# The start of a hybrid decoder layer: two weight loads split on VectorE alone, and 18 transposes of the identity on TensorE

## The chip, the cores and the metric

The kernel runs on one core of a Trainium2 chip. The metric is the device time of one execution in microseconds (us); the time before is the median of three runs.

## The reference, cut to what matters

One layer over 512 tokens of width 1024, float32: token mixing with two groups of heads that share one input projection, then cross-attention, then a squared-ReLU MLP. The change lies in the first lines of the mixing:

```python
h = rmsnorm(x, norm_mix_g[l])
proj = h @ w_in[l]
p_qn, p_qr, p_ckv, p_kr, p_qi, p_ki, p_wi, p_qkv = jnp.split(proj, split_at, axis=-1)
...
c_kv = rmsnorm(p_ckv, kv_norm_g[l])
k_rope = rope(p_kr[:, :, None, :])[:, :, 0]
q_idx = rope(p_qi.reshape(B, S, IDX_HEADS, IDX_DIM))
k_idx = rope(p_ki[:, :, None, :])[:, :, 0]
```

The latent keys `c_kv`, the small rotary keys, the index keys and index weights (232 columns together) come first, then the 512 index queries. They feed the indexer, whose top-128 choice of keys restricts the attention of group A.

## The kernel before, in words

The 512 tokens are four tiles of 128 rows. Each float32 operand of a product is split into a high part `hi` (a cast on ScalarE, line 130 for weights, 230 for activations) and a rest `lo` (a subtraction, line 131 or 231), and a product is made of three passes: hi by hi, hi by lo, lo by hi (`mm3`, line 107 issues them). Eight row blocks of 128 make the inner dimension, so one tile's product has 24 steps.

`load_weight` fetches a weight in units into the tag `wraw` (three buffers), splits each into `whi` and `wlo` (six buffers each), and takes a letter for each unit that says on which engine the subtraction runs: "p" is GpSimd and "v" VectorE, with the cast on ScalarE in both. A weight of at most 256 columns has two units of four row blocks, a wider one four units of two row blocks.

The start goes as follows. GpSimd makes the identity. SP issues the first rows of x, the gains, the first weight `wa` (232 columns, two units) with the remaining rows between its units, then tables, then the second weight `wb` (512 columns, four units). For each token tile, eight transposes (line 113) put its columns into PSUM, lines 230 and 231 make the two parts of `hT`, and line 267 sums the squares of the row (`junk`), from which GpSimd gets `r_mix` (line 200). Then for each tile the product with `wa` is made in a bank of the tag `mm` (three buffers) and evacuated: a mean square on ScalarE (line 205), `rk` on GpSimd (line 200), `ctok`, eight rotary products (line 289), two sums (line 296), a copy and `weff` on VectorE, and three transposes that are split into `cT`, `kiT` and `krT`. Then the query products with `wb` for tiles 1 to 3 in the same banks, their rotary products, and the index products, whose relu is weighted and summed on VectorE (lines 375 and 377). Further on come the weights of group B (`wv` with "vpvp", queries and keys with "pppp"), the choice of the top 128 (lines 557 and 558, VectorE), the two attentions, the cross-attention and the MLP. The bank of the tag `pv` (one buffer) is first used by the attention of group B.

The order on each engine isn't written out here: a planner simulates the engines with costs of its own and takes of the ready instructions the one that comes first in the program. Each engine then runs its list in that order. Only later parts (from the output projection on) hold TensorE to the program's order.

Of the kernel before, what the change touches and what calls it, by code (L numbers as in the profile page):

```python
# [17 lines left out]
P = 128  # L18
# [5 lines left out]
NH = 8  # L24
DH = 64
DR = 32
# [12 lines left out]
C_QN, C_QR, C_CKV, C_KR, C_QI, C_KI, C_WI, C_QB, C_KB, C_VB = (  # L39
    0, 512, 768, 896, 928, 1440, 1504, 1512, 2024, 2536)  # L40
# [24 lines left out]
def kernel(  # L65
# [16 lines left out]
    def nm(s):  # L82
        uid[0] += 1
        return f"{s}_{uid[0]}"

    def mtile(shape, dt, tag, bufs=1, pool=None):
        return (pool or main).tile(shape, dt, name=nm(tag), tag=tag, bufs=bufs)

    def small(tag, n=1):
        return main.tile([P, n], F32, name=nm(tag), tag=tag, bufs=8)  # L90

    def bank(tag, bufs):
        return psp.tile([P, 512], F32, name=nm(tag), tag=tag, bufs=bufs)
# [18 lines left out]
    def tpose(*a, **k):  # L112
        ins = nc.tensor.transpose(*a, **k)  # L113
        if ordered[0]:
            tc.keep_in_program_order(ins)

    ident = main.tile([P, P], F32, name="ident")
# [6 lines left out]
    def split_unit(raw, hi, lo, how="v"):  # L124


        if how in "PV":
            nc.vector.tensor_copy(hi, raw)  # L128
        else:
            nc.scalar.copy(hi, raw)  # L130
        (nc.gpsimd if how in "pP" else nc.vector).tensor_tensor(lo, raw, f32(hi), op=ALU.subtract)  # L131

    def load_weight(w, segs, k0, how, between=None):


        n = sum(c1 - c0 for c0, c1 in segs)
        nk = 4 if n <= 256 else 2
        his, los = [], []
        for u in range(KD // nk):
            raw = mtile([P, nk, n], F32, "wraw", 3)  # L140
            hi = mtile([P, nk, n], F32R, "whi", 6)
            lo = mtile([P, nk, n], F32R, "wlo", 6)
            rows = w[(k0 + nk * u) * P:(k0 + nk * u + nk) * P, :].rearrange("(k p) c -> p k c", p=P)
            o = 0
            for c0, c1 in segs:
                nc.sync.dma_start(raw[:, :, o:o + c1 - c0], rows[:, :, c0:c1])
                o += c1 - c0
            split_unit(raw, hi, lo, how[u % 4])
            if between is not None:
                between(u)  # L150
            for j in range(nk):
                his.append(hi[:, j, :])
                los.append(lo[:, j, :])
        return his, los
# [44 lines left out]
    def rstd_of(mean_eps, dst):  # L199
        nc.gpsimd.tensor_tensor(dst, mean_eps, mhalf, op=ALU.pow)  # L200
# [19 lines left out]
    def transpose_half(rows, g0, his, los, bank=bank_tp):  # L220

        tps = [bank()[:, :2 * P].rearrange("p (j t) -> p j t", j=2) for _ in range(2)]
        for i in range(2):
            for j in range(2):
                tpose(tps[i][:, j, :], rows[:, (2 * i + j) * P:(2 * i + j + 1) * P], ident)
        for j in range(2):
            for i in range(2):
                c = 2 * i + j
                g = gT[:, g0 + c:g0 + c + 1]
                nc.scalar.activation(his[c], tps[i][:, j, :], AF.Copy, scale=g)  # L230
                nc.vector.scalar_tensor_tensor(los[c], tps[i][:, j, :], g, f32(his[c]), op0=ALU.mult, op1=ALU.subtract)  # L231
# [3 lines left out]
    att = p1b.enter_context(tc.tile_pool(name="att", bufs=1, side="right"))  # L235
    tmp = p1a.enter_context(tc.tile_pool(name="tmp1", bufs=1))

    xa = [mtile([P, 2, D], F32, f"u2{c}") for c in "ab"]
    nc.sync.dma_start(xa[0][:, 0, 0:512], x_rows[:, 0, 0:512])
    load_gains([norm_mix_g], G_MIX)  # L240
    nc.sync.dma_start(xa[0][:, 0, 512:], x_rows[:, 0, 512:])
    w_in0 = w_in[0]

    def x_load(t):
        nc.sync.dma_start(xa[t // 2][:, t % 2, :], x_rows[:, t, :])

    wa = load_weight(w_in0, [(C_CKV, C_KR + DR), (C_KI, C_WI + NH)], 0, "vpvp", between=lambda u: x_load(1 + u))
    x_load(3)
    tabs = tmp.tile([P, CONST_COLS - 640], F32, name="tabs")
    nc.sync.dma_start(tabs, consts[:, 640:])  # L250
# [7 lines left out]
    for t in range(NT):  # L258
        xt = xa[t // 2][:, t % 2, :]
        tsl = slice(t * P, (t + 1) * P)  # L260
        for h in range(2):
            transpose_half(xt[:, 512 * h:512 * h + 512], G_MIX + 4 * h,
                           [hT[0][:, 4 * h + j, tsl] for j in range(4)],
                           [hT[1][:, 4 * h + j, tsl] for j in range(4)], (bank_tp, bank_s)[h])
        junk = att.tile([P, D], BF16, name=nm("junk"), tag="p", bufs=3)
        ss = small("ss")
        nc.vector.tensor_tensor_reduce(junk, xt, xt, op0=ALU.mult, op1=ALU.add, scale=1.0 / D, scalar=EPS, accum_out=ss)
        rstd_of(ss, r_mix[:, t:t + 1])
# [69 lines left out]


    qiT = mtile([P, NH, 3, P], F32R, "u1")  # L340
    wb = load_weight(w_in0, [(C_QI, C_QI + 512)], 0, "pppp")
    for t in range(1, NT):
        ps = bank_mm()
        mm3(ps, h_tok(t), wb)
# [19 lines left out]
    for b in range(1, NT):  # L364
        n = P * (b + 1)
# [630 lines left out]
```

## Time and profile before

| what | value |
|---|---|
| median of three runs | 813.85 us (813.5 to 816.56) |
| profiled execution, its own time | 814.07 us |
| its span, first to last instruction | 812.3 us |
| TensorE products busy | 785.9 us, 97% |
| VectorE busy | 560.0 us, 69% |
| ScalarE busy | 382.5 us, 47% |
| GpSimd busy | 215.4 us, 27% |

The engines are PE (TensorE products), PEld (its weight loads), DVE (VectorE), ACT (ScalarE), POOL (GpSimd) and SP (the queue that issues most transfers). Times in the trace count from the start of the span. A busy share is a mean over the whole span. A timeline row gives the start, the time from the start of the first to the end of the last instruction merged into it, the engine, the line, the operation, what it writes and reads, its shape and its count; the brackets give the idle time before it and what ended it. `whi`, `wlo` and `wraw` are the parts of a weight, `h` both parts of `hT`.

### The profile page before, as it was taken

Reading aid. Unit: us, or ns where it says so; the run is one execution under the profiler, and the core shown is the slowest. Engines: PE = TensorE matmul, PEld = TensorE weight load, DVE = VectorE, ACT = ScalarE, POOL = GpSimd, SP = SyncE. Lnnn points to the kernel's source line nnn. Section 1 sums busy time; section 2 is a strip of 40 time slices with the busy share of each in tenths; the row PEclk is TensorE's granted clock in tenths of the full one; section 3 lists DMA queues with packets and bytes.
Section 4 is the critical chain, followed back from the end, with each engine's and each line's share of the span. In section 5 each row is a group of like instructions: output and inputs, shape, how many; then the busy total and the mean of one; then the engine's idle time right before and its main releaser. Section 6 shows DMA issues by size and latency. Waiting matters only on the chain.

```text
span 812.3 us, 11144 instructions
## 1 busy us (share of the span) xinstructions
PE 785.9 (97%) x4066; PEld 649.0 (80%) x4066; DVE 560.0 (69%) x1169; ACT 382.5 (47%) x743; POOL 215.4 (27%) x164
## 2 busy tenths in 40 slices
PE   6799999999999999999999999999999999999995
PEld 5688878985698778788898888888888888888884
DVE  6775999998668844634683447767776776676674
ACT  5444333457955634222472545533552455345544
POOL 4733143130613406544510201110111011201132
PEclk9899999999999999999999999999999999999998
DMA  8441232202423303322540333496439743963482
GB/s 288 133 119 38 69 105 73 66 1 78 156 79 105 105 1 103 102 80 79 181 140 18 103 104 82 101 229 212 99 83 209 225 100 85 223 221 85 89 164 103
DMA packets 53223, 94.12 MB, mean 116 GB/s; under 512 B 5265, under 2 KB 11057, under 8 KB 53169
## 3 DMA queue, kind: packets, MB, share of 16 engines
q1 hardware_dynamic: 44464, 76.64, 30.1%
q0 software_dynamic: 8704, 16.78, 12.4%
q8 instruction: 32, 0.52, 0.3%
q14 instruction: 23, 0.18, 0.1%
HBM read 90.78 MB, written 2.10 MB: 114 GB/s over the span
## 4 chain that ended last, share of the span: by engine, by line
PE 82%; DVE 10%; issue 3%; POOL 2%; ACT 2%; DMA 1%; SPq 0%; POOLq 0%; ACTq 0%; DVEq 0%
PE mm L107 61%; PE sc L107 11%; PE tp L113 5%; PE pv L107 3%; PE tp L107 2%; DVE glo L558 1%; DVE m L557 1%; DVE ghi L377 1%; ACT whi L130 1%; DMA u2b<-in_w_down_dram 1%; DVE whi L128 1%; DVE rb L289 1%; DVE kk L296 0%; DMA u2a<-in_x_dram 0%; DVE wlo L131 0%
## 5 line engine op out<-in xcount | busy, mean ns | idle before, releaser
L131 POOL TENSOR_TENSOR wlo<-wraw,whi 128x1024 fp32r<-128x1024 f32 (+2 forms) x59 | 139.3, 2379 | 186.8 <-ACT whi L130 156.7
L107 PE MATMUL mm<-whi,h 128*128 128x512 f32 (+2 forms) x536 | 165.3, 377 | 6.9 <-DVE h L231 3.5
L130 ACT CAST whi<-wraw 128x1024 fp32r<-128x1024 f32 (+3 forms) x111 | 114.0, 1029 | 93.9 <-PE mm L107 42.4
L107 PE MATMUL mm<-h,whi 128*128 128x512 f32 (+1 forms) x448 | 153.2, 366 | 0.0
L107 PE MATMUL mm<-u,whi 128*128 128x512 f32 x320 | 125.0, 390 | 0.0
L107 PE MATMUL mm<-u,wlo 128*128 128x512 f32 x320 | 124.7, 390 | 0.0
L107 PEld LDWEIGHTS mm<-whi,h 128*128 128x128 f32 x536 | 100.6, 194 | 21.6 <-DVE h L231 3.9
L107 PE MATMUL mm<-wlo,h 128*128 128x512 f32 (+2 forms) x280 | 104.9, 376 | 0.1
L131 DVE TENSOR_TENSOR wlo<-wraw,whi 128x1024 fp32r<-128x1024 f32 (+1 forms) x64 | 80.6, 1260 | 29.7 <-ACT whi L130 29.4
L107 PEld LDWEIGHTS mm<-h,whi 128*128 128x128 f32 x448 | 80.7, 188 | 14.7 <-issue 1.2
L895 POOL DMA_DIRECT2D u2b<-in_w_down_dram x24 | 32.6, 1369 | 224.5 <-DMA wraw<-in_w_down_dram 120.6
L107 PE MATMUL mm<-whi,ghi 128*128 128x512 f32 x192 | 76.2, 397 | 0.0
L107 PE MATMUL mm<-wlo,ghi 128*128 128x512 f32 x192 | 75.7, 394 | 0.0
L107 PE MATMUL mm<-whi,glo 128*128 128x512 f32 x192 | 75.1, 391 | 0.0
L107 PEld LDWEIGHTS mm<-u,wlo 128*128 128x128 f32 x320 | 60.1, 188 | 12.5
L107 PEld LDWEIGHTS mm<-u,whi 128*128 128x128 f32 x320 | 60.1, 188 | 12.2
L131 DVE TENSOR_TENSOR wlo<-u2b,whi 128x1024 fp32r<-128x1024 f32 x32 | 39.1, 1225 | 30.2 <-ACT whi L130 30.2
L107 PEld LDWEIGHTS mm<-wlo,h 128*128 128x128 f32 x280 | 54.1, 194 | 7.2 <-DVE wlo L131 0.5
L130 ACT CAST whi<-u2b 128x1024 fp32r<-128x1024 f32 x32 | 33.6, 1052 | 48.0 <-DMA u2b<-in_w_down_dram 39.5
L428 ACT ACTIVATE p<-p,mx 128x128 f32<-128x128 f32 (+3 forms) x64 | 35.9, 563 | 26.4 <-DVE mx L426 26.3
L862 ACT ACTIVATE sq<-r 128x512 f32<-128x512 f32 x32 | 20.2, 631 | 49.1 <-DVE r L860 49.1
L860 DVE SCALAR_TENSOR_TENSOR r<-mm,rT 128x512 f32<-128x512 f32 x32 | 22.0, 688 | 30.3 <-PE mm L107 23.2
(250 smaller groups left out, 1433.7 us busy)
## 6 DMA issues: line engine op xcount, KB each, us to landing
wraw<-in_w_up_dram SPq DMA_DIRECT2D x32, 512.0 KB, 4.7
wraw<-in_w_down_dram SPq DMA_DIRECT2D x24, 512.0 KB, 6.1
u2b<-in_w_down_dram POOLq DMA_DIRECT2D x24, 512.0 KB, 7.6
wraw<-in_w_in_dram SPq DMA_DIRECT2D x16, 512.0 KB, 4.0
wraw<-in_w_kv_cross_dram SPq DMA_DIRECT2D x16, 512.0 KB, 3.7
wraw<-in_w_out_dram SPq DMA_DIRECT2D x8, 512.0 KB, 3.8
wraw<-in_w_q_cross_dram SPq DMA_DIRECT2D x8, 512.0 KB, 3.7
wraw<-in_w_o_cross_dram SPq DMA_DIRECT2D x8, 512.0 KB, 3.7
```

The lines of the kernel that those rows point to most:

```text
L107: ins = nc.tensor.matmul(*a, **k)
L113: ins = nc.tensor.transpose(*a, **k)
L128: nc.vector.tensor_copy(hi, raw)
L130: nc.scalar.copy(hi, raw)
L131: (nc.gpsimd if how in "pP" else nc.vector).tensor_tensor(lo, raw, f32(hi), op=ALU.subtract)
L289: nc.vector.scalar_tensor_tensor(o, i, r, tab, op0=ALU.mult, op1=ALU.mult)
L377: nc.vector.scalar_tensor_tensor(acc[b], rl[:, :n], wh, acc[b], op0=ALU.mult, op1=ALU.add)
L428: nc.scalar.activation(pr[:, c], pr[:, c], AF.Exp, bias=mx[:, i:i + 1], scale=-1.0, accum_out=sm[:, i:i + 1])
L557: nc.vector.max(m8, acc[b])
L860: nc.vector.scalar_tensor_tensor(r, ps, 0.0, rows_ready[0], op0=ALU.max, op1=ALU.mult)
L862: nc.scalar.activation(sq, r, AF.Square)
L895: nc.gpsimd.dma_start(xw[:, u], src, accum_op=ALU.add)
```

## The change

`load_weight` for `wa` and for `wb` gets "v" for every unit. A bank of the tag `pv` is taken at the start, and `busy(n)` writes n transposes of the identity into its four quarters in turn: 10 before the first rows are asked for in the program's order, and 8 after the transposes of token tile 0. Nothing reads that bank.

```diff
@@ -235,6 +235,14 @@
     tmp = p1a.enter_context(tc.tile_pool(name="tmp1", bufs=1))
+    idle = bank("pv", 1)
+
+    def busy(n):
+        for i in range(n):
+            tpose(idle[:, (i % 4) * P:(i % 4 + 1) * P], ident, ident)
+
+    busy(10)
     xa = [mtile([P, 2, D], F32, f"u2{c}") for c in "ab"]
@@ -244,7 +252,7 @@
-    wa = load_weight(w_in0, [(C_CKV, C_KR + DR), (C_KI, C_WI + NH)], 0, "vpvp", between=lambda u: x_load(1 + u))
+    wa = load_weight(w_in0, [(C_CKV, C_KR + DR), (C_KI, C_WI + NH)], 0, "vvvv", between=lambda u: x_load(1 + u))
@@ -262,6 +270,8 @@
                            [hT[1][:, 4 * h + j, tsl] for j in range(4)], (bank_tp, bank_s)[h])
+        if t == 0:
+            busy(8)
         junk = att.tile([P, D], BF16, name=nm("junk"), tag="p", bufs=3)
@@ -338,7 +348,7 @@
-    wb = load_weight(w_in0, [(C_QI, C_QI + 512)], 0, "pppp")
+    wb = load_weight(w_in0, [(C_QI, C_QI + 512)], 0, "vvvv")
```

## Rows read from the trace of the kernel before

**Rows 1.** What TensorE waited for, 0 to 60 us: total, times, longest.
```profile
PE tp L113 <- DMA u2a<-in_x_dram: 3.7, 1, 3.7
PE mm L107 <- DVE h L231: 3.5, 1, 3.5
...
PE mm L107 <- DVE weff L329: 1.0, 1, 1.0
```

**Rows 2.** Busy time by stretch: us, PE, PEld, DVE, ACT, POOL, clock, DMA, GB/s.
```profile
80.00:180.00 100.00, 98.49 (x541) 83.81 (x541) 98.62 (x296) 42.06 (x93) 32.87 (x18) 1.00 0.23 65
180.00:215.00 35.00, 32.98 (x192) 19.79 (x189) 27.48 (x88) 28.41 (x73) 8.47 (x4) 0.96 0.33 99
```

**Rows 3.** The same view in slices of one microsecond.
```profile
24.00:25.00 1.00, 0.00 (x0) 0.00 (x0) 1.00 (x4) 0.09 (x1) 0.79 (x2) 0.60 0.92 338
...
30.00:31.00 1.00, 1.00 (x7) 0.99 (x6) 0.22 (x1) 0.62 (x2) 0.86 (x2) 0.50 0.00 0
```

**Rows 4.** The timeline of TensorE, 0 to 30 us.
```profile
5.14 1.11 PE L113 MATMUL sc<-ident,u2a 128*128 128x128 f32 x4
8.45 0.56 PE L107 MATMUL mm<-whi,h 128*128 128x232 f32 x1 [2.19 <-ACT whi L130]
...
12.10 0.42 PE L107 MATMUL mm<-wlo,h 128*128 128x232 f32 x1
...
14.19 0.28 PE L107 MATMUL mm<-wlo,h 128*128 128x232 f32 x1
...
25.55 0.56 PE L107 MATMUL mm<-whi,h 128*128 128x232 f32 x1 [3.46 <-DVE h L231]
...
27.39 0.42 PE L107 MATMUL mm<-wlo,h 128*128 128x232 f32 x1
```

**Rows 5.** The timeline of VectorE, 10 to 36 us, and one row at 75 us.
```profile
11.65 3.16 DVE L267 CUSTOM_DVE_ANT_0 junk<-u2b 128x1024 bf16<-128x1024 f32 x1
...
15.00 1.23 DVE L267 CUSTOM_DVE_ANT_0 junk<-u2b 128x1024 bf16<-128x1024 f32 x1
...
18.86 0.35 DVE L321 SCALAR_TENSOR_TENSOR ctok<-mm,rk,gkvr 128x128 f32<-128x128 f32 x1 [0.45 <-POOL rk L200]
...
20.33 0.35 DVE L231 SCALAR_TENSOR_TENSOR h<-tp,gT,h 128x128 fp32r<-128x128 f32 x1
20.59 4.03 DVE L296 TENSOR_TENSOR kk<-kk,rb 128x64 f32<-128x64 f32 x2
...
34.47 1.22 DVE L131 TENSOR_TENSOR wlo<-wraw,whi 128x1024 fp32r<-128x1024 f32 x1
35.60 0.35 DVE L296 TENSOR_TENSOR kk<-kk,rb 128x64 f32<-128x64 f32 x2
...
75.01 2.44 DVE L377 SCALAR_TENSOR_TENSOR glo<-rl,weff,glo 128x256 f32<-128x256 f32 x1 [2.53 <-ACT rl L372]
```

**Rows 6.** The timeline of GpSimd, 0 to 31 us.
```profile
1.01 0.28 POOL masks.py:199 TENSOR_SCALAR_AFFINE_SELECT ident<-ident 128x128 f32<-128x128 f32 x1
...
11.58 2.15 POOL L131 TENSOR_TENSOR wlo<-wraw,whi 128x928 fp32r<-128x928 f32 x1
...
19.91 4.66 POOL L131 TENSOR_TENSOR wlo<-wraw,whi 128x1024 fp32r<-128x1024 f32 x2
...
27.96 2.37 POOL L131 TENSOR_TENSOR wlo<-wraw,whi 128x1024 fp32r<-128x1024 f32 x1 [3.09 <-ACT whi L130]
30.29 0.57 POOL L200 TENSOR_TENSOR rk<-rstd,mhalf 128x1 f32<-128x1 f32 x1
```

**Rows 7.** The chain that ended last, at the first query product: start, us, what.
```profile
34.70 5.72 PE mm L107 x24
```

**Rows 8.** SP's queue, a row of the timeline from 20 to 33 us.
```profile
22.30 8.42 SPq L146 DMA_DIRECT2D wraw<-in_w_in_dram  x3
```

**Rows 9.** The page: a group of part 5, and part 6 (KB each, us to landing).
```profile
L130 ACT CAST whi<-wraw 128x1024 fp32r<-128x1024 f32 (+3 forms) x111 | 114.0, 1029 | 93.9 <-PE mm L107 42.4
...
wraw<-in_w_in_dram SPq DMA_DIRECT2D x16, 512.0 KB, 4.0
```

## The prediction, made before the kernel was timed

> **What bounds the kernel now.** I read the page first, then the list of what TensorE waits for, the long table by stages, the one-microsecond table of the start, and last each engine's own order there. The page's busy shares are means over stages with different limits, so they say little about a change in the start. The list of waits says where TensorE's idle time is: of what it waits for in the first 60 us, nearly all comes before 35 us: 3.7 us for the first rows, 3.5 us for a VectorE instruction, 1.0 us for a bank [rows 1], and 2.2 us for the first weights [rows 4]. From 80 to 180 us it idles 1.5 us, from 180 to 215 us 2.0 us [rows 2]. There is something to gain in the first 35 us, then, and it reaches the end only if the stretch from 80 to 215 us doesn't take it back.
>
> In the first 35 us the reader should see three things. First, TensorE is slow up to about 14 us and again from 25.5 to 31 us. The clock column shows the second stretch: it falls within the slice 24 to 25 us, after TensorE has idled since about 22 us, and is still at 0.50 (1.2 GHz) from 30 to 31 us. A product of 232 columns with "wlo" takes 0.42 us there (27.39). At 12.10 it also takes 0.42 us, and at 14.19 0.28 us [rows 3, 4]. The column shows nothing of the first stretch; I trust the length of the products and put the rise between 12.1 and 14.2 us.
>
> Second, the 3.5 us of idle time hang on one VectorE pair, the sums "kk" of line 296. It lasts 4.03 us at 20.59, and 0.35 us at 35.60. It ends at 24.6 us, when GpSimd's two subtractions of line 131, begun at 19.91, end. The row sum "junk" at 11.65 lasts 3.16 us, at 15.00 only 1.23 us; a GpSimd subtraction ran from 11.58 to 13.73 us there [rows 5, 6]. A VectorE instruction that reads PSUM, line 231 at 20.33, ran through.
>
> Third, the bank that TensorE waits for at 34.70 us becomes free with "weff" of token tile 1 [rows 1, 7]. That evacuation needs tile 1's "rk" from GpSimd, which starts at 30.29 us, right behind the subtraction of 27.96 us [rows 6].
>
> **What the change removes.** "wa" has only two units (232 columns go four row blocks at a time), so "vpvp" held one GpSimd split; "wb" held four. Five subtractions leave GpSimd: one of 2.15 us, two of 4.66 us together, and two of about 2.37 us, 11.6 us in all [rows 6]. With them go, on VectorE, the surplus at the two blocked places: 3.16 - 1.23 = 1.9 us and 4.03 - 0.35 = 3.7 us, 5.6 us together [rows 5]. VectorE gets five subtractions: the one at 34.47 lets the next instruction start 1.13 us later, so four such are 4.5 us and one of 928 in place of 1024 columns is 1.0 us, 5.5 us together [rows 5]. VectorE's total stays as it is; what changes is its order, and TensorE's idle time and clock.
>
> The Trainium skill, page "SBUF — State Buffer", section "SBUF: two separate sides", says that VectorE and GpSimd share one pair of ports under an exclusive lock, which a VectorE instruction with two SBUF inputs needs too. The rows of lines 296 and 267 agree, and by that rule both blocked places vanish.
>
> TensorE's side. Without the block, 3.5 us of idle time go. The stretch from 25.55 to 31.0 us, busy at half rate, gives 2.7 us back. The bank wait gives up to 1.0 us. If the clock rises before the first product at 8.45 us, what is done until 12.1 or 14.2 us takes half: 1.8 to 2.9 us if TensorE is busy all that time [rows 1, 3, 4]. I take 2.4 us; that makes 9.6 us as the upper end.
>
> VectorE's side. By 11.65 us it has finished tile 0's eight "h" and one of tile 1. Before tile 1's "weff" it must still do two row sums (2.4 us at 1.2), the second "wa" split (1.0), 23 "h" of line 231 at 0.26 us (20.33 to 20.59; 6.0), tile 0's evacuation and that of tile 1 up to weff. From ctok at 18.86 us to the end of the eight rotary products at 20.33 us it is 1.47 us; the two sums add 0.35 us, and a copy and two small splits 0.8 us if I cost them like an "h". So tile 0 takes 2.6 us, and tile 1 1.6 us with weff [rows 5]. The sum is 13.6 us, which gives 25.3 us at the earliest, against 34.5 us now: 9.2 us gained. If all four "wb" splits come ahead of weff, it is 29.8 us: 4.7 us gained. The planner fills VectorE's idle time with them, so some will come ahead: I take two, 2.3 us, and the 0.45 us that VectorE waited for tile 0's rk [rows 5]. That is 28.1 us, a gain of 6.4 us, below TensorE's upper end, so VectorE sets it.
>
> The raw buffers. "wraw" has three, so the fourth "wb" unit is fetched when the first has been split: the first of the two merged GpSimd splits ends at 22.2 us, and SP goes on at 22.30 [rows 6, 8]. From there it is 4.0 us to landing, 1.03 us for the cast [rows 9] and 1.13 us for the split: 6.2 us. The query product needs that unit after 18 of its 24 steps, which take 5.72 us: 4.3 us after its start [rows 7]. If VectorE has split the first unit by 26 us, a product begun at 28.1 us waits for nothing.
>
> What is added. Ten transposes need only the identity, ready at 1.3 us [rows 6]. Four took 1.11 us at 5.14 us, some 0.4 us of it the last one's own length, so about 0.23 us each [rows 4]: ten end at 3.6 us, before the first rows at 3.75 us [rows 1]. The other eight, 1.8 us, fit into the idle time before 8.45 us (2.2 us). If the planner puts them ahead of tile 0, which needs its rows while they need none, tile 0's transposes come up to 1.8 us later, and the same 2.2 us cover that. I take nothing, and bound it by 0 and 1.8 us. Their bank, "pv", is used next by the attention of group B, far behind on the same engine. If they don't raise the clock, they cost nothing under this cover and bring nothing.
>
> The Trainium skill, page "TensorE: Matmul & The Clock Gate", Part 4, says that transposes don't count as TensorE activity for its clock in the way products do; it speaks against this part. No stretch of this trace holds transposes alone for long enough to tell. By that rule the 2.4 us fall out, and 7.2 us are left as TensorE's upper end.
>
> **The sum.** The profiled execution took 814.07 us (its span of 812.3 us and 1.8 us around it), 0.2 us above the median of 813.85 us. Off go 6.4 us at the start of the query products. I give back 1.1 us: the two "wb" splits left for later are 2.3 us of VectorE's time inside TensorE's query products, and I let half of it become waits. Gain 5.3 us, so 808.5 us from the median. From the query products on TensorE has almost no idle time up to 180 us, so the shift is carried. The likeliest case's own range is 804.6 us (9.2 us gained) to 810.5 us (4.7 us, less the leak and a little for order).
>
> **Rivals.**
> 1. The transposes don't lift the clock. A "wlo" product still takes 0.42 us up to about 12 us. Of 2.4 us I count 2.0 us as lost, since VectorE limits that stretch too: 810.5 us. For it speaks only the absence of a row to the contrary.
> 2. VectorE becomes the bound: all four splits come ahead of weff, or the first comes so late that the fourth unit's 6.2 us end behind the query product. Then the gain is 4.7 us less about 2.3 us of new waits: 811.5 us. For it: VectorE has few microseconds to spare there; against it: "h" and evacuations come first in the program.
> 3. The gain is taken back later. VectorE is busy 98.6 of 100 us between 80 and 180 us [rows 2]. If its work in there doesn't start earlier, TensorE waits the more for it between 180 and 215 us: 813.9 us. Against it: that work starts from index products of TensorE, which move forward with the rest.
> 4. Slower: the blocking moves instead of going. GpSimd keeps two splits of "wv" and all of the query and key weights of group B, and an index sum at 75.01 us, 256 columns wide, is held 2.44 us as it is [rows 5]. If the new order lets these splits meet VectorE's two-input work more often, VectorE has its 5.5 us more and no relief, with 1.4 us free from 80 to 180 us [rows 2]. TensorE then comes out of that stretch up to 5.5 us late: 819.4 us. It decides from about 4 us of new blocking on.
>
> **Chances.** Forecast 0.55, rival 1 0.12, rival 2 0.13, rival 3 0.12, rival 4 0.08. About 0.5% (4.1 us) is what a measurement of this kernel tells from no change, so faster means under 809.8 us. Of the forecast 0.50 lies there, of rival 1 0.05; rivals 2 and 3 and what is left of these two lie within; slower takes rival 4 and 0.01 of rival 3. That is 0.55, 0.36 and 0.09. The range takes in the upper end of the gain and rival 3, and leaves out rival 4 and the edges: 804.8 to 814.2 us.
>
> **What would show it.** Right: no wait over 1 us for a VectorE "h" in the first 30 us; no 0.50 in the clock column there; a "wlo" product of 0.28 us at 10 us already; the pair of line 296 under 0.5 us throughout; the first query product of 512 columns at 25 to 30 us. Wrong: that product later than 32 us, a fall of the clock while TensorE waits for splits, or TensorE's idle time between 180 and 215 us grown by what the start gained. The weakest step is the count of splits put ahead of weff, since that order is the planner's.

## The result and the profile after

| | before | after |
|---|---|---|
| median of 8 runs each, us | 814.59 (813.46 to 816.56) | 822.90 (815.14 to 824.92) |
| ratio, with its 95% interval | | 1.0078 [1.0059, 1.0097] |
| profiled execution, us | 814.07 | 823.06 |
| its span, us, and mean granted clock | 812.3, 0.990 | 821.3, 0.979 |

The kernel became slower by 0.8%; 808.5 us was forecast, in a range of 804.8 to 814.2. After's eight runs aren't spread evenly. Two, with a mean clock of 0.990 and 0.992, took 816.95 and 815.14 us; the other six, with 0.978 to 0.982, took 822.65 to 824.92 us. The profiled execution is one of the six.

**The start.** What TensorE waited for from 0 to 60 us of after (total, times, longest), to be held against [rows 1]:

```profile
PE tp L113 <- DVE h L231: 2.5, 4, 1.0
PE mm L107 <- ACT h L230: 2.2, 1, 2.2
PE pv L113 <- POOL ident masks.py:199: 1.4, 1, 1.4
```

The waits of 3.7 us for rows, of 3.5 us for one VectorE "h" and of 1.0 us for "weff" are gone. The wait for rows only gave way to the transposes of the identity: tile 0's own transposes come later, at 5.24 us instead of 3.75. What is left for "h" comes in pieces of at most 1.0 us, and VectorE's timeline in after shows why (start, us):

```profile
13.29 1.21 DVE L277 CUSTOM_DVE_ANT_0 junk<-u2b 128x1024 bf16<-128x1024 f32 x1
...
17.56 1.23 DVE L131 TENSOR_TENSOR wlo<-wraw,whi 128x1024 fp32r<-128x1024 f32 x1 [0.29 <-ACT whi L130]
...
21.57 1.22 DVE L131 TENSOR_TENSOR wlo<-wraw,whi 128x1024 fp32r<-128x1024 f32 x1
...
23.22 0.21 DVE L306 TENSOR_TENSOR kk<-kk,rb 128x64 f32<-128x64 f32 x1
...
23.97 1.22 DVE L131 TENSOR_TENSOR wlo<-wraw,whi 128x1024 fp32r<-128x1024 f32 x1
...
25.47 1.21 DVE L131 TENSOR_TENSOR wlo<-wraw,whi 128x1024 fp32r<-128x1024 f32 x1
...
29.10 0.21 DVE L339 TENSOR_SCALAR weff<-mm,r_mix 128x8 f32<-128x8 f32 x1
```

The row sum takes 1.21 us where it took 3.16, the pair "kk" 0.21 (at 23.22) and 0.18 us (at 23.61) where it took 4.03 [rows 5]. That is what the Trainium skill, page "SBUF — State Buffer", section "SBUF: two separate sides", would have, and this trace agrees. All four "wb" splits stand ahead of weff. TensorE's timeline in after:

```profile
1.35 4.10 PE L113 MATMUL pv<-ident 128*128 128x128 f32 x18 [1.35 <-POOL ident masks.py:199]
5.24 0.54 PE L113 MATMUL tp<-ident,u2a 128*128 128x128 f32 x3
...
6.03 0.60 PE L113 MATMUL sc<-ident,u2a 128*128 128x128 f32 x4
8.80 0.56 PE L107 MATMUL mm<-whi,h 128*128 128x232 f32 x1 [2.17 <-ACT h L230]
...
10.71 0.41 PE L107 MATMUL mm<-wlo,h 128*128 128x232 f32 x1
...
29.62 0.39 PE L107 MATMUL mm<-whi,h 128*128 128x512 f32 x1
```

The planner put all 18 transposes ahead of tile 0's. Behind them four transposes of rows take 0.60 us (at 6.03), where four took 1.11 us in before [rows 4]: the engine ran fast by then, though it had done nothing but transposes. Then it idles 2.17 us, and the first products are as slow as before (0.56 us; "wlo" 0.41 us at 10.71). One-microsecond slices of after (columns as in [rows 2]) show it, and a second fall like the one in [rows 3]:

```profile
8.00:9.00 1.00, 0.20 (x1) 0.20 (x1) 0.49 (x1) 1.00 (x4) 0.00 (x0) 0.87 1.16 353
9.00:10.00 1.00, 0.67 (x2) 0.40 (x3) 1.00 (x3) 0.59 (x4) 0.00 (x0) 0.50 1.07 367
...
26.00:27.00 1.00, 1.00 (x7) 1.00 (x6) 1.00 (x3) 0.39 (x2) 1.00 (x1) 0.50 0.75 94
```

**How much the start gained.** The first query product of 512 columns begins at 29.62 us instead of 34.70 [rows 7], 5.1 us earlier. But that overstates it, as TensorE's groups of instructions up to that product show. Before, up to 34.69 us:

```profile
L107 PE MATMUL mm<-whi,h 128*128 128x232 f32 x64 | 17.5, 353 | 5.9 <-DVE h L231 3.5 <-ACT whi L130 2.2 <-ACT h L230 0.2
L107 PE MATMUL mm<-wlo,h 128*128 128x232 f32 x32 | 10.1, 323 | 0.1
...
L113 PE MATMUL sc<-ident,u2b 128*128 128x128 f32 x8 | 2.0, 346 | 0.0
```

After, up to 29.61 us:

```profile
L107 PE MATMUL mm<-whi,h 128*128 128x232 f32 x50 | 13.9, 362 | 2.4 <-ACT h L230 2.2 <-DVE h L231 0.2
L107 PE MATMUL mm<-wlo,h 128*128 128x232 f32 x26 | 8.7, 337 | 0.3 <-DVE wlo L131 0.3
...
L113 PE MATMUL sc<-ident,u2b 128*128 128x128 f32 x6 | 1.4, 330 | 0.6 <-DVE h L231 0.6
```

Of 96 products with "wa" only 76 lie ahead of it: 20 were moved behind. So were six transposes, two of the last rows and the first two each of "ctok" and, in its two widths, "kk". At 0.11 us each at full rate (two products from 29.28 to 29.50 us, a transpose of "ctok" from 34.16 to 34.27) these 26 are 2.9 us. By this estimate the start gained about 2.2 us.

**Where it goes.** The next milestone is the last of the index products with 256 columns, which starts VectorE's work on the choice of the top 128. In before it begins at 74.12 us, in after at 77.94. The same view up to those times, before (to 74.1 us):

```profile
L107 PE MATMUL mm<-whi,h 128*128 128x512 f32 x102 | 33.4, 396 | 1.0 <-DVE weff L329 1.0
L107 PE MATMUL mm<-wlo,h 128*128 128x512 f32 x51 | 20.3, 398 | 0.0
```

and after (to 77.9 us):

```profile
L107 PE MATMUL mm<-whi,h 128*128 128x512 f32 x119 | 38.3, 395 | 0.0
L107 PE MATMUL mm<-wlo,h 128*128 128x512 f32 x60 | 23.6, 393 | 0.0
```

TensorE does 179 products of 512 columns before it, where it did 153. 72 of them are query products in both; the others are products for group B, which the program has behind the index products. The planner took 81 of these first in before already, all with "wv", and 107 in after: the 96 with "wv" and 11 with the next weight (by the lists that e5 and e6 hold, below). At 5.72/24 = 0.24 us [rows 7] the 26 more are 6.2 us: 6.2 less the 2.2 gained is 4.0, and 3.8 us is measured. VectorE's work on the top 128 starts 2.8 us late and ends 8.6 us late, as its first and last "m" show, before:

```profile
79.89 0.43 DVE L557 MAX8 m<-glo 128x8 f32<-128x256 f32 x1
...
179.68 0.69 DVE L557 MAX8 m<-ghi 128x8 f32<-128x512 f32 x1
```

and after:

```profile
82.66 0.43 DVE L567 MAX8 m<-glo 128x8 f32<-128x256 f32 x1
...
188.23 0.67 DVE L567 MAX8 m<-ghi 128x8 f32<-128x512 f32 x1
```

Ahead of its last rounds after does scores of group B's attention on VectorE (line 436, from 185.03 us on) that before has behind them (line 426, from 185.51 us on). The same stretches as in [rows 2], of after, and the one behind them:

```profile
80.00:180.00 100.00, 97.11 (x548) 82.96 (x547) 98.93 (x289) 41.94 (x94) 30.44 (x17) 1.00 0.21 59
180.00:215.00 35.00, 32.54 (x149) 18.75 (x148) 25.24 (x84) 22.47 (x58) 3.42 (x2) 0.76 0.21 61
215.00:250.00 35.00, 33.91 (x254) 27.12 (x253) 24.28 (x87) 24.50 (x66) 10.90 (x5) 0.95 0.37 121
```

VectorE has as little free time as before (1.1 us of 100), so it doesn't make up its delay; TensorE idles 2.9 us there instead of 1.5. In the second stretch the clock column falls from 0.96 to 0.76: 0.20 x 35 = 7.0 us of full-rate work. In slices of two microseconds, after:

```profile
184.00:186.00 2.00, 0.77 (x3) 0.50 (x4) 2.00 (x8) 1.42 (x4) 0.00 (x0) 1.00 0.94 175
186.00:188.00 2.00, 2.00 (x7) 0.97 (x6) 2.00 (x9) 1.25 (x5) 0.00 (x0) 0.56 0.95 253
...
196.00:198.00 2.00, 2.00 (x6) 0.72 (x4) 0.91 (x3) 0.00 (x0) 0.00 (x0) 0.50 0.00 0
...
202.00:204.00 2.00, 2.00 (x8) 0.73 (x8) 1.10 (x5) 2.00 (x7) 0.00 (x0) 0.67 0.00 0
```

TensorE is busy 0.77 of the 2 us before 186 us, then the clock falls to 0.50 and stays there about 17 us, although TensorE is busy. The wait in front of the fall is one for VectorE (TensorE's timeline of after), in the first scores of the attention:

```profile
184.15 0.41 PE L113 MATMUL mm<-ident,ghi 128*128 128x128 f32 x2 [0.46 <-DVE rb L299]
185.64 1.09 PE L107 MATMUL sc<-u2b,u2a 64*128 64x384 f32 x2 [1.08 <-DVE mx L436]
```

In before the same product begins behind 0.49 us of waiting for "mx", and its slice from 184 to 186 us is busy 1.31 us. The first scores themselves aren't late (182.78 us, in before 183.98): TensorE had done other work ahead. So the loss is best counted on TensorE, as an estimate from the rows above. From 80 to 250 us it idles 2.9 us more than before (1.4, 0.4 and 1.1; before has none in the third stretch) and loses 8.8 us more to the clock (7.0, and 0.05 x 35 = 1.8). Less the 2.2 us that the start gained, that is 9.5 us, near the 9.0 us by which the span grew. The clock is the greater part by far.

### The profile page after: what moved, and what is told of

Same layout as the page of the kernel before. It is cut to its first block, busy times and chain, and to the rows that moved or that the text cites. A ratio compares the mean times of both kernels' runs of the same rounds, so it can differ in the third digit from the quotient of the medians.

```text
span 821.3 us, 11197 instructions
## 1 busy us (share of the span) xinstructions
PE 796.3 (97%) x4084; PEld 655.2 (80%) x4084; DVE 560.7 (68%) x1174; ACT 383.9 (47%) x743; POOL 204.0 (25%) x159
## 4 chain that ended last, share of the span: by engine, by line
PE 70%; DVE 19%; issue 4%; DMA 3%; ACT 2%; POOL 1%; SPq 0%; POOLq 0%; ACTq 0%
PE mm L107 50%; PE sc L107 11%; PE tp L113 4%; DVE m L567 3%; PE pv L107 2%; DVE ghi L568 2%; PE tp L107 2%; DMA u2b<-in_w_down_dram 2%; DVE rb L299 2%; DMA wraw<-in_w_in_dram 1%; DVE ghi L387 1%; DVE tok L299 1%; DVE wlo L131 1%; DVE glo L568 1%; DVE tok L306 1%
## 5 line engine op out<-in xcount | busy, mean ns | idle before, releaser
L131 POOL TENSOR_TENSOR wlo<-wraw,whi 128x1024 fp32r<-128x1024 f32 (+1 forms) x54 | 127.3, 2374 | 198.8 <-ACT whi L130 168.2
L107 PEld LDWEIGHTS mm<-whi,h 128*128 128x128 f32 x536 | 99.8, 194 | 16.5 <-ACT h L230 2.6
L131 DVE TENSOR_TENSOR wlo<-wraw,whi 128x1024 fp32r<-128x1024 f32 (+2 forms) x69 | 86.9, 1260 | 31.0 <-ACT whi L130 31.0
L107 PEld LDWEIGHTS mm<-u,whi 128*128 128x128 f32 x320 | 60.1, 188 | 12.3
```

The lines of the kernel that those rows point to most:

```text
L107: ins = nc.tensor.matmul(*a, **k)
```

## The experiments

Three theories were open when the trace of after had been read. **Theory 1:** the gain at the start is real, and the planner's other order of TensorE's instructions takes it back. **Theory 2:** the transposes cost it. **Theory 3:** VectorE's five added subtractions are the loss, whatever the order. "Q" is the start of the first query product, "I" that of the last index product of 256 columns, both in the profiled execution. The kernel before ran beside each group of kernels: 815.04 us beside the first four, 815.33 beside the next four, 815.53 beside the last three (medians of 29). e2 has six runs, e6 five, e8 eleven, the others twelve each.

| kernel | median, us | ratio to before, 95% | Q, us | I, us | I - Q |
|---|---|---|---|---|---|
| before | | | 34.70 | 74.12 | 39.4 |
| after | 822.90 | 1.0078 [1.0059, 1.0097] | 29.62 | 77.94 | 48.3 |
| e1_wa_only | 811.81 | 0.9974 [0.9953, 0.9995] | 30.74 | 70.16 | 39.4 |
| e2_wb_only | 822.12 | 1.0091 [1.0075, 1.0107] | 26.51 | 76.75 | 50.2 |
| e3_splits_only | 820.85 | 1.0055 [1.0032, 1.0078] | 27.65 | 77.33 | 49.7 |
| e4_busy_only | 815.88 | 1.0018 [1.0004, 1.0032] | 33.09 | 74.59 | 41.5 |
| e5_splits_old_order | 812.95 | 0.9964 [0.9942, 0.9985] | 30.98 | 70.42 | 39.4 |
| e6_before_new_order | 827.67 | 1.0143 [1.0112, 1.0175] | 32.04 | 84.11 | 52.1 |
| e7_after_old_order | 817.26 | 1.0022 [1.0001, 1.0042] | 34.22 | 73.66 | 39.4 |
| e8_after_bridge | 816.24 | 1.0008 [0.9991, 1.0024] | 35.57 | 75.02 | 39.5 |
| e9_bridge_all_order | 814.87 | 0.9988 [0.9968, 1.0008] | 32.05 | 71.47 | 39.4 |
| e10_wb_one_unit | 813.64 | 0.9977 [0.9959, 0.9996] | 32.95 | 72.37 | 39.4 |
| e11_wb_two_units | 823.27 | 1.0087 [1.006, 1.0114] | 29.44 | 77.86 | 48.4 |

The last column is the one to read first. Where TensorE has before's list from there on, 39.4 to 39.5 us lie between the two products whatever else is changed; where it has the one with 26 more products ahead, 48.3 to 52.1. (e4's list is one product shorter than before's there; its 41.5 us hold 5 us at a clock of 0.50.) VectorE follows: from its first "m" to its last it is 99.7 to 99.8 us with the first kind of list, and 105.6 to 105.7 us with the second (e4: 103.9).

**The parts, each alone.** e1 changes the letters of "wa", e2 those of "wb", e3 both, and e4 adds only the transposes (the edits here and below are shortened).

```diff
 e1, e3:  wa = load_weight(..., 0, "vpvp" -> "vvvv", ...)
 e2, e3:  wb = load_weight(..., 0, "pppp" -> "vvvv")
 e4:      idle, busy(n), busy(10), busy(8) as in the change; "vpvp" and "pppp" stay
```

> Only the second unit of the 232-column weight goes to VectorE; the query weight stays on GpSimd, and there are no transposes of the identity. TensorE's list is then the one of before, instruction for instruction. If the loss comes from the new order of TensorE's list (theory 1), this kernel has none of it: 812 to 814.6 us, at most 2 us faster, because one of the two blocked places of VectorE (the row sum at 11.65 us) goes. If the loss comes from the transposes (theory 2), the same. If VectorE's added work is the loss (theory 3): 1 us slower, about 815.5 us.

> Only the query weight goes to VectorE. TensorE's list then has the index products of the first block behind some 13,300 more columns of other products than before (125,184 columns ahead of the eighth in place of 111,872; the change has the same). Theory 1 (order): the first query product comes at 29 to 31 us, 4 to 5 us earlier, but the eighth index product at 76 to 79 us, no earlier than the 74 us of before; time 814 to 823 us, not faster. Theory 2 (the transposes cost it): 808 to 811 us. Theory 3 (VectorE's added 4.5 us): about 819 us wherever the index products stand.

> Both splits as in the change, none of the transposes. Theory 1: as the run with the query weight alone, whose TensorE order it shares at the index products: 813 to 823 us. Theory 2: 808.5 us as forecast, since what costs is gone. Theory 3: 820 us.

> The 18 transposes alone, splits as before. The index products stand within 1,800 columns of their old place (113,664 ahead of the eighth, 2,304 of them the transposes). Theory 1: 813 to 816 us, the clock rising near 5 us and falling again in the idle gap before the first weights. Theory 2: 818 us or more. Theory 3: no change, 814.6 us.

Measured: e1 is faster, e2 and e3 are slower, e4 lies 0.8 us above before. So the loss comes with "wb" and needs no transposes. e1's TensorE list is that of before, and its start carries through to the last index product (TensorE's timeline of e1):

```profile
30.74 0.47 PE L107 MATMUL mm<-whi,h 128*128 128x512 f32 x1 [1.05 <-DVE weff L329]
...
70.16 0.40 PE L107 MATMUL sc<-glo,u 128*128 128x256 f32 x2
```

4.0 us earlier at both places. That is more than the 2 us expected, because both of VectorE's blocked places went and not one: GpSimd keeps its four splits of "wb", but the sums "kk" took 0.40 and 0.17 us (at 20.17 and 21.01), at the end of one split of 2.38 us and right before the next. So the relief there was a matter of timing. e2's Q, too, came earlier than expected (26.51 us, not 29 to 31), and its I did not (76.75 us). Two of e1's twelve runs took 817.9 and 818.1 us, with a mean clock of 0.983 where the others have 0.991 to 0.996. e3's list, like after's, has 179 products of 512 columns ahead of the index product. e3 also prices the clock. Its profiled execution didn't have the long fall (two-microsecond slices of e3):

```profile
184.00:186.00 2.00, 0.98 (x3) 0.44 (x4) 2.00 (x10) 1.68 (x6) 0.00 (x0) 1.00 0.92 168
186.00:188.00 2.00, 2.00 (x11) 1.10 (x11) 2.00 (x8) 1.55 (x5) 0.00 (x0) 1.00 0.98 336
```

and took 815.21 us. Of e3's twelve runs the five with a mean clock of 0.989 or more took 814.46 to 818.38 us, the seven with 0.985 or less 820.46 to 823.76 us: 4.7 us between the two medians. In e2 all six runs lie at 0.981 to 0.985. Only the profiled runs have a trace, so that the fall at 186 us is what separates the others is inferred from their mean clock. What speaks for it: the waits in front of the scores, 0.46 and 1.08 us in after, are 0.45 to 0.47 and 1.08 us in e2, e3, e6 and e11 as well, and the clock falls to 0.50 behind them in after, e2, e6 and (for about 7 us) e11; of the 43 runs of these five kernels 32 have a mean clock of 0.985 or less, of the 87 of before beside the experiments five. What speaks against it as the whole of it: e3's profile has the same waits and no fall, and e7 (below), with before's list on TensorE, has as low a mean clock in eight of its twelve runs.

**The order alone.** e5 makes both splits on VectorE and holds TensorE to before's list; e6 keeps before's work and holds TensorE to e3's list. Both do so with ordering edges inside one engine that make nothing wait. (In e5 to e9 the same lines have higher numbers, since the list stands at the head of the file.)

```diff
+    order = [traced[n] for n in places]        # e5: before's list, e6: that of e3
+    for a, b in zip(order, order[1:]):
+        tc.add_manual_dep(b, a.name, DependencyInfo(NoSync, DATA), reason="given order")
 e5:  "vvvv" for wa and wb       e6:  "vpvp" and "pppp" as before
```

> Both splits as in the change, no transposes of the identity, and TensorE held by dependencies to the list of the kernel before, instruction for instruction. Theory 1 (the new order of TensorE's list eats the gain): the first query product at 26 to 30 us, the eighth index product at 67 to 70 us in place of 74, VectorE's dense stretch starts 4 to 6 us earlier; 806 to 811 us. Theory 3 (VectorE's 5.5 us of added work is the loss): 817 to 821 us, since the work is the same.

> The kernel before, with its splits on GpSimd and no transposes, but TensorE held to the list that the planner makes for the two splits on VectorE. Theory 1: the start as before (first query product at 33 to 36 us), the eighth index product 3 to 6 us later than 74 us, 817 to 823 us, slower than before although nothing is added to any engine. Theory 3: 814.6 us, as before.

Measured: the same splits are 7.9 us faster in the old order (812.95 against 820.85 us; the intervals of the ratios don't meet), and the new order alone costs before 12.3 us. Against the five runs of e3 at the higher clock (median 817.30 us) 4.4 of the 7.9 us are left; the rest goes with the clock. (The two were run in different groups, between which before moved by 0.3 us.) This settles it between theories 1 and 3: VectorE has its five subtractions in e5, and the kernel is 0.4% faster than before. The planner makes the other engines' lists around TensorE's, so it is TensorE's list with what follows from it that costs. The two timelines of TensorE, e5:

```profile
30.98 0.47 PE L124 MATMUL mm<-whi,h 128*128 128x512 f32 x1
...
70.42 0.40 PE L124 MATMUL sc<-glo,u 128*128 128x256 f32 x2
```

and e6:

```profile
32.04 0.77 PE L124 MATMUL mm<-whi,h 128*128 128x512 f32 x1 [3.06 <-DVE weff L348]
...
84.11 0.40 PE L124 MATMUL sc<-glo,u 128*128 128x256 f32 x2
```

e6 reaches I 10.0 us late, more than the 3 to 6 expected and than the 6.2 us of the 26 products: the list was made for splits on VectorE, and with GpSimd's TensorE waits 3.6 us for "weff" where it waited 1.0. So e6 shows that the order alone can cost; how much of its 12.3 us after shares, it doesn't show. Its slices show 0.50 for 13.7 us from 194 us on too. e5 stayed short of what was expected of it (806 to 811 us): Q is at 30.98 us, not 28.1, because waits for VectorE's "h" are left in the old order, one of 1.4 us and three of 1.3 us together, and 3.4 us are spent at a clock of 0.5 around 25 us.

**How little of "wb" is enough.** With "wa" on VectorE, e10 gives one of wb's four units to VectorE, e11 two.

```diff
 e10:  wa "vvvv", wb "vppp"
 e11:  wa "vvvv", wb "vpvp"
```

> The 232-column weight on VectorE and one of the four units of the query weight (vppp), no transposes. The planner leaves the index products in their old places (111,872 columns ahead of the eighth). Theory 1: 810 to 813.5 us, as with the first weight alone or a little faster, faster than before. Theory 3: 1 us slower than with the first weight alone, 813 us.

> As the run before with two of the four units on VectorE (vpvp). The planner now moves the index products 13,312 columns back, as with all four. Theory 1: a jump, 815 to 823 us, the eighth index product at 76 us or later. Theory 3: 1 us more than with one unit.

Measured: 813.64 and 823.27 us, a step of 9.6 us for one more subtraction of 1.2 us. With one unit I - Q is that of before, with two it is longer by 9.0 us. (e11's Q stands in a merged row that begins with a product of 232 columns.) The cost follows the list, not VectorE's load.

**The transposes.** e7 is the whole change with TensorE held to 18 transposes and then before's list; e8 moves 8 of them behind tile 0's own; e9 is e8 with ScalarE, VectorE and GpSimd held to e5's lists as well.

```diff
 e7:  fill[0:18], then before's list
 e8:  fill[0:10], tile 0's transposes, fill[10:18], then the rest of before's list
 e9:  as e8, and the lists of ScalarE, VectorE and GpSimd taken from e5
```

> The change with all of its parts, the 18 transposes first on TensorE as the planner put them, then the list of the kernel before. Theory 1: as the splits alone with this list, plus up to 1.5 us for tile 0's later transposes: 807 to 812 us. Theory 2 (the transposes cost several us by the fall of the clock behind them): 812 to 816 us, 4 us or more behind the splits alone.

> As the run before, but the last eight transposes of the identity stand behind tile 0's own, where the source has them, so that they fill the idle time before the first weights. If transposes raise and hold the clock: products of 232 columns at the upper level (0.28 us with wlo) from 9 us on, and 1 to 2 us faster than with all 18 in front: 806 to 810 us. If what follows the first weights is too sparse to hold it, the clock falls again before 14 us and the two kernels agree within 1 us.

> The change with the last eight transposes behind tile 0's, and now ScalarE, VectorE and GpSimd too held to the lists that they had in the run of the splits alone with TensorE's old list (812.95 us, first query product at 30.98 us). If the transposes cost their 3 to 4 us through the lists that the planner changes on ScalarE (the weight's cast before tile 0's h parts), this kernel has none of it: first query product at 29 to 31 us, 810 to 813.5 us. If the transposes themselves cost it, by TensorE's time or its clock, it stays at 815 to 817 us, first query product at 34 to 36 us.

Measured: 4.3, 3.3 and 1.9 us above e5. e7 lies above what either theory gave it, e8 1.0 us from e7, as expected if the clock isn't held, and e9 between its two cases. The intervals of e7 and e8 don't meet that of e5; e9's meets both e5's and e8's, so its place between them isn't shown. No arrangement of the transposes gained anything in this start. e7's profile is of its fastest run (814.19 us): eight of its twelve have a mean clock of 0.985 or less (median 818.29 us; the other four 814.83), and none of e5's has. So a part of e7's 4.3 us is clock, with before's list on TensorE, and no trace shows where it fell. TensorE's timeline of e7:

```profile
1.35 3.70 PE L131 MATMUL pv<-ident 128*128 128x128 f32 x18 [1.35 <-POOL ident masks.py:199]
4.89 0.49 PE L131 MATMUL tp<-ident,u2a 128*128 128x128 f32 x3
...
8.76 0.56 PE L124 MATMUL mm<-whi,h 128*128 128x232 f32 x1 [2.52 <-ACT h L249]
12.09 0.69 PE L131 MATMUL tp<-ident,u2a 128*128 128x128 f32 x2 [2.77 <-DVE h L250]
```

As in after, the clock is up behind the transposes, and down again after 2.52 us of idle time (0.56 us for the first product). That idle time ends with a ScalarE "h" which starts at 8.34 us, behind the cast of the first weight; in e5 ScalarE has its first two "h" at 5.07 us and the cast behind them. e9 takes that away, and it has no wait over 1.4 us; still its "wlo" products take 0.41 us up to 12.10 us and 0.27 at 14.06, as in before [rows 4] and e5. Its transposes are in two parts with tile 0's rows between them, and four transposes of rows at 5.33 us take 1.11 us, as in before; the last eight of the identity end at 8.15 us, and the first product still runs at the lower rate (TensorE's timeline of e9):

```profile
8.45 0.56 PE L153 MATMUL mm<-whi,h 128*128 128x232 f32 x1 [0.30 <-ACT whi L178]
```

e9's Q lies 1.1 us behind e5's; whether the other 0.8 us are real, the runs don't tell.

e4 is the one place where the transposes did what was hoped (its timeline of TensorE):

```profile
7.96 0.38 PE L107 MATMUL mm<-whi,h 128*128 128x232 f32 x1 [0.43 <-ACT h L230]
...
9.73 0.27 PE L107 MATMUL mm<-wlo,h 128*128 128x232 f32 x1
```

The idle time is 0.43 us, and the first products run fast, from 8 to 10 us. Behind a wait of 1.29 us for "h" the clock column is at 0.50 from 11 to 14 us. Q comes 1.6 us earlier. Then TensorE waits 2.3 us for "ctok" and 1.0 us for "weff" around 30 us, the clock is at 0.50 for 6.8 us, and at I the kernel is 0.5 us late.

## Why the prediction was wrong, step by step

- **Five subtractions leave GpSimd, and VectorE's two blocked places vanish.** Right, by the rows of VectorE above: 5.6 us less blocking. Rival 4 isn't the cause: VectorE's busy time over the whole run is 560.7 us against 560.0, so the five subtractions (5.5 us) and the relief (5.6) cancel as the prediction had it, and there is no room for 4 us of new blocking. The index sum at 79.62 us is held 2.68 us, as one of before was 2.44 us [rows 5].
- **First query product at 28.1 us.** 29.62 was measured, within the range of 25.3 to 29.8. The mis-sized term is the count of "wb" splits ahead of weff: four, not two, and for four the text had worked out 29.8 us.
- **The gain of 6.4 us.** Mis-sized, because the milestone was taken as if TensorE had done the same work up to it. 20 products and six transposes were put behind it; about 2.2 us of gain are left in after. In e1 and e5, where the list stays, it is 4.0 and 3.7 us.
- **The transposes cost nothing and bring 2.4 us.** They don't bring it here. Alone they add 0.8 us (e4); with the splits and the old order 4.3 and 3.3 us (e7 and e8 against e5; in e7 a part of it is clock). That a part of it comes through the lists of the other engines (e8 against e9: 1.4 us) fits ScalarE's order in e7, but lies within the intervals and isn't shown. The cover named for them, the idle time before 8.45 us, wasn't cover: it was as long as before (2.17 us), because ScalarE's first "h" came behind the cast (at 8.38 us, in before at 5.06), and in it the clock fell. Rival 1 named this outcome, though for another reason: in after the clock does rise after transposes.
- **"From the query products on TensorE has almost no idle time up to 180 us, so the shift is carried."** This is the step that failed. In these runs a busy engine carried a shift only where its list stayed the same. The 26 products put ahead hold the index products, and with them VectorE, back by 6.2 us, more than the start gained; what was then to be carried was a delay of 3.8 us. e5 shows the gain kept without the new order (I at 70.42 us, 0.9964), e3 the same splits with it (77.33 us, 1.0055), and e6 the new order without the splits (84.11 us, 1.0143).
- **Rival 3** named the place: VectorE's stretch doesn't start earlier, and TensorE waits the more for it (1.4 us more from 80 to 180 us, 0.4 from 180 to 215). Its counter-argument, that the index products "move forward with the rest", is what fell: they moved back 3.8 us. Its price ended at no gain; what it lacked was the clock, which fell behind that wait and cost some 7 us more.
- **Theory 3** falls with e5 and e10: the same load in the old order is faster than before, and one subtraction of 1.2 us less than e11's takes 9.6 us off.

That the new order is the cause is shown, by e5 against e3 and by the step from e10 to e11. That it acts through the wait and the clock is read from the profiles: the wait stands in all five with that list, the fall behind it in four. What else decides on the fall stays open, and so does why the planner changes its choice at the second "wb" unit.

Three versions come out ahead of before: e1, one string changed, 0.9974 [0.9953, 0.9995], e10, 0.9977 [0.9959, 0.9996], and e5, 0.9964 [0.9942, 0.9985]. The intervals overlap, so none is shown to be the best, and all three gains are below the 0.5% of the prediction's bound.

## What to carry to other kernels

Where a planner orders the instructions, an edit has two prices: its own work, and the list that the planner makes of everything else. Compare each engine's list before summing durations, count the work ahead of a milestone before calling it earlier, and move work from engine to engine in single units or with the old order held. A small new wait for a full engine may cost little itself and much through the clock behind it; here half a microsecond more of waiting stood in front of 17 us at half rate.

## What the runs showed of the hardware

- Transposes alone raised TensorE's clock in three profiles: behind 18 of them (4.10 us) three transposes of rows took 0.54 us in after and, behind 3.70 us, 0.49 us in e7, 0.87 us without them in before; in e4 these three still took 0.84 us, but the first product, behind nothing but transposes, 0.38 us where it took 0.56. The Trainium skill, page "TensorE: Matmul & The Clock Gate", Part 4, has it that transposes don't count like products; these rows don't agree, and they decide. But in e8 and e9, with 10 and 8 of them around tile 0's, TensorE did nothing but transposes from 1.35 to 8 us and the first product took 0.56 us: what makes the difference isn't shown. The rise didn't last through 2.17 us of idle time in after.
- The clock stayed at 0.50 for about 17 us from 186 us on with TensorE busy in nearly every slice, in scores with 64 rows and transposes, and e3's profiled execution, with the same waits in front, went without that fall. For this kernel the difference is 4.7 us between e3's two sets of runs and 6.9 us between after's (medians of 823.0 and 816.0 us).
